# Four edits to the planner that orders a hybrid decoder step: product prices, a page slack, the moment of weight loads, a held accumulator

## The chip, the cores and the metric

The kernel runs on one core of one Trainium2 chip. The metric is device time in microseconds (us) of one launch, lower is better. The kernel before took 855.02 us as the median of three runs (854.64 to 855.18).

## What is computed

One layer of a decoder step for a prompt of 256 tokens and for 8 requests of 8 new tokens each, 320 token columns in all. Everything is float32. Cut to what matters here:

```python
z = x @ w_in                                    # 2048 x 8272, split among three head groups
# A: sparse attention, 8 heads x 128; an indexer scores all keys, the best 256 (64) are attended
sc  = sum_h w[t,h] * relu(q_idx[t,h] . k_idx[s]);  sel = top_k(sc)
a   = softmax(q . K[sel]) @ V[sel]              # for requests: K and V in 16 pages of 128 tokens each
# B: gated linear recurrence, 4 heads x 128
S_t = diag(f_t) S_{t-1} + outer(1 - f_t, i_t);  b = S_t^T q_t
# M: attention over 256 memory tokens, 4 heads; for the prompt their keys and values are products too
m   = softmax(q . mk) @ mv
y   = concat(a * silu(.), norm(b) * silu(.), m * silu(.)) @ w_out      # 2048 x 2048
out = layernorm(alpha * x + y)
```

The new keys, values, index keys, states and memory keys and values are outputs as well.

## The kernel before, in words

**Products.** TensorE multiplies in a fast float32 form. For accuracy each operand is split into a high and a low part (`xh`, `xl` for the activations, `wh`, `wl` for the weights), and each product is made of three: high by high, low by high, high by low. A weight tile of 128 x 1024 is loaded by SyncE's queue (SP) into one of three raw buffers `wr`; ScalarE casts each half of it to `wh`, VectorE or GpSimd subtracts to get `wl` (four buffers each, so four halves); then TensorE uses the half, which frees the buffer. One weight tile of the input projection gives 24 products of 320 columns (256 columns for the indexer's queries), in four quanta of six products. Order of the weights: a first block, queries, keys, values, the recurrence's inputs, gates, the memory weights (16 tiles, products of 512 and 256 columns), the memory queries, the last gates, and then the output projection in four chunks of 512 columns.

**Pages.** The requests' cached keys and values are read as pages of 128 x 1024. A "unit" is four pages, held in two buffers of the tag `pg` (five buffers) or `S` (three, shared with the score rows); TensorE reads the pages as moving operand of small matmuls, into the PSUM bank `kv` for scores and `va` for values. There are 68 units: eight for the keys and eight for the values of each of four request pairs, and four for the memory caches. TensorE visits them two at a time where it can.

**The order is written at build time by a planner.** The class `Plan` keeps a clock for each engine, for the SP queue and for the DMAs. Each instruction that the program emits is charged a cost (`Engine.cost`, line 188) and moves that engine's clock; `plan.w` and `plan.r` hold when each buffer was last written and read. The main loop goes step by step at `plan.now`, which follows TensorE's clock:

- `loads()` (line 2057) puts DMAs on SP's queue: a weight tile first if a raw buffer is about to be free (line 2065, up to 1 us ahead of it), then stores, then pages if a page buffer is free and the planned DMA clock is less than 4 us ahead.
- the weights' halves are prepared when they have landed and a `wh` buffer is free.
- `background()` (line 2021) advances generators (attention, recurrence, softmax and so on), each of which emits small matmuls, VectorE and ScalarE work when its inputs count as ready.
- then TensorE gets either a visit of one or two page units (`units_now`, line 800) or a quantum of products (`pe_quantum`, line 1686). If neither counts as ready, `plan.now` moves by 0.1 us and nothing is emitted.

So the planner's clock decides only the order of the instructions on each engine and queue. On the chip each engine runs its list in that order and waits on semaphores where the data are not there yet.

The helpers that the change touches: `unit_ready` (line 779) and `loaded` (line 797) say whether a unit's pages count as landed; `slot_free(tag, bufs)` (line 89) gives the planned time from which a new buffer of a tag may be taken, infinite if the buffers are pinned; `unit` (line 722) emits a unit's matmuls and for values takes the bank `va` at the first of eight units; `extract` (line 1262) reads that bank when all eight are done.

Of the kernel before, what the change touches and what calls it, by code (L numbers as in the profile page):

```python
# [45 lines left out]
HASTE = 2.0  # L46
CALM = 4.0
IDLE = 3.0
LOOK = 3
TABLES = {AF.Exp: "exp_ln", AF.Ln: "exp_ln", AF.Silu: "silu", AF.Sqrt: "sqrt"}  # L50
EXP_LN = 6
# [94 lines left out]
class Engine:  # L146
# [41 lines left out]
    def cost(self, op, outs, ins, n):  # L188
        if self.name == "PE":
            n, a = math.prod(outs[0].shape[1:]), ins[0]  # L190
            shape = tuple(next(w for w in (32, 64, 128) if m <= w) for m in (a.shape[0], math.prod(a.shape[1:])))
            turn = 0.0
            if shape != self.shape:
                turn = 0.31 if shape == (128, 128) else 0.09 if self.shape == (128, 128) else 0.2
                self.shape = shape
            if op == "transpose":
                return turn + 0.109
            if a.dtype == F32R:
                return turn + 0.0087 + n * 0.0004325
            if a.dtype == BF:  # L200
                return turn + max(0.06, n / 2400 + 0.003)
            if shape == (128, 32):
                return turn + max(0.028, n / 2400)
            return turn + 2 * max(0.109, n / 1200 + 0.002) * (0.5 if shape[0] == 64 else 1)
        scalars = sum(math.prod(x.shape[1:]) == 1 for x in ins) if n > 1 else 0
        sb = all(x.space != bass.MemoryType.PSUM for x in outs + ins)
        if self.name == "ACT":
            return ((112 if sb else 62) + n) / 1200 + 0.09 * scalars + (0.1 if len(outs) > 1 else 0)
        if self.name == "POOL":
            return (130 + 0.75 * n) / 960 if op in ("memset", "tensor_copy", "iota") else (170 + 2.0 * n) / 960  # L210
        f = 1.0
        if op in ("max", "match_replace"):
            return (66 + n) / 960 - 0.05
        if op == "tensor_tensor_scan":
            f = 2.0
        elif op in ("tensor_copy", "tensor_scalar", "memset") and sb:
            f = 0.55
        elif op == "reciprocal":
            f = 6.0
        return (66 + n * f) / 960 + 0.055 * scalars  # L220
# [8 lines left out]
def hymba_step(ctx: ExitStack, tc: tile.TileContext, I, O):  # L229
    nc = tc.nc  # L230
    plan = Plan()
# [60 lines left out]
    def PS(shape, which=None, dt=F32):  # L292
        if which is None:
            fa, fb = [(held[w] == 2, plan.slot_free(w, 2)) for w in ("mA", "mB")]
            which = "mA" if fa <= fb else "mB"
        return new(shape, which, dt, psum)
# [220 lines left out]
    wspec = []  # L517
# [204 lines left out]
    def unit(n):  # L722
        kind, p, u = punits[n]
        tl = [PG.pop((n, b)) for b in range(2)]
        plan.pinned.difference_update(t.tensor.name for t in tl)
        in_s.difference_update([(n, 0), (n, 1)])
        if kind == "K":
            if u == 0:
                S[p] = new([128, PAST + NS], "S")
                plan.pinned.add(S[p].tensor.name)  # L730
            if u % 2 == 0:
                st["kv"] = PS([128, 512], "kv")
            c = 256 * (u % 2)
            for hh in range(2):
                for h2 in range(2):
                    for b, hp, g in GROUPS:
                        h = 4 * hh + 2 * hp + h2
                        PE.matmul(st["kv"][g:g + 32, c:c + 256], st["qpad"][:, h, 2 * p + b, :],
                                  tl[b][:, :, 128 * h:128 * h + 128], start=hh == h2 == 0, stop=hh == h2 == 1)
            if u % 2:  # L740
                ps = st.pop("kv")
                plan.pinned.add(ps.tensor.name)
                bg.insert(0, [key_scores(p, u, ps), need(ps, ps=0)])
        elif kind == "V":
            if u == 0:
                VACC[p] = PS([128, 512], "va")
            for j in range(2):
                kt = 2 * u + j
                for b, hp, g in GROUPS:
                    PE.matmul(VACC[p][g:g + 32, :], PTt[p][:, kt, g:g + 32], pair(tl[b][:, j, :], hp),  # L750
                              start=kt == 0, stop=False)
            if u == 7:
                for b, hp, g in GROUPS:
                    PE.matmul(VACC[p][g:g + 32, :], PTt[p][:, 16, g:g + 32], pair(avS, hp),
                              start=False, stop=True)
                bg.insert(0, [extract(p), need(VACC[p], ps=0)])
                done.add(("vdone", p))
        elif kind == "XK":
            if p == 0:
                st["xk"] = PS([128, 512], "kv")  # L760
            ps = st["xk"][:, 256 * p:256 * p + 256]
            for h in range(4):
                for b in range(4):
                    PE.matmul(ps[32 * b:32 * b + 32, :], st["mqpad"][:, 4 * p + b, h, :],
                              tl[b // 2][:, b % 2, 256 * h:256 * h + 256], start=h == 0, stop=h == 3)
            if p == 1:
                for g in range(2):
                    bg.insert(0, [xsoft(g, st["xk"][:, 256 * g:256 * g + 256]), need(st["xk"], ps=0)])
        else:
            va = PS([128, 512], ("va", "kv")[p])  # L770
            for nt in range(2):
                for b in range(4):
                    PE.matmul(va[32 * b:32 * b + 32, :], st["xpt", p][:, nt, 32 * b:32 * b + 32],
                              tl[b // 2][:, b % 2, 512 * nt:512 * nt + 512], start=nt == 0, stop=nt == 1)
            bg.insert(0, [xextract(p, va), need(va, ps=0)])
            if p == 1:
                free(st["mqpad"])

    def unit_ready(n):
        kind, p, u = punits[n]  # L780
        if any((n, b) not in PG or plan.avail(PG[n, b]) > plan.now for b in range(2)):
            return False
        if kind == "K":
            return u % 2 or ("aq", 7) in done and plan.slot_free("kv", 1) <= plan.now and (
                u or plan.slot_free("S", BUFS["S"]) <= plan.now and len(S) + len(in_s) + ci_live(1) < BUFS["S"]
                and (p < BUFS["S"] or ("soft", p - BUFS["S"]) in done))
        if kind == "V":
            return ("soft", p) in done and plan.avail(PTt[p]) <= plan.now and (u < 7 or "attn" in done) and (
                u or plan.slot_free("va", 1) <= plan.now)
        if kind == "XK":  # L790
            return p or "mqpad" in done and "kv" not in st and plan.slot_free("kv", 1) <= plan.now
        return p or ("attn" in done and all(("xsoft", g) in done and plan.avail(st["xpt", g]) <= plan.now for g in (0, 1))
                     and max(plan.slot_free("va", 1), plan.slot_free("kv", 1)) <= plan.now)
# [1 line left out]
    since = [None]  # L795

    def loaded(n):
        return all((n, b) in PG and plan.avail(PG[n, b]) <= plan.now for b in range(2))

    def units_now(n):  # L800

# [460 lines left out]
    def extract(p):  # L1262
        while not has_room(2):
            yield
        o = [T(256), T(256)]
        for i in range(2):
            ACT.activation(o[i], VACC[p][:, 256 * i:256 * i + 256], AF.Copy, scale=RS[p][:, 1:2])
        del VACC[p], PTt[p]
        yield from wait(("gate", 7))
        yield need(*o)  # L1270
        ps = PS([128, 4, 128])
        for h4 in range(4):
            PE.transpose(ps[:, h4, :], o[h4 // 2][:, 128 * (h4 % 2):128 * (h4 % 2) + 128], ident)
        pv = ps.rearrange("p a (b h m q) -> p a b h m q", b=2, h=2, m=4)
        cv = st["cat"][0][:, 0:8, 256 + 16 * p:272 + 16 * p].rearrange("p (a h m) (b q) -> p a m b h q", a=2, h=2, b=2)
        for h4 in range(4):
            d = cv[:, h4 // 2, h4 % 2]
            DVE.tensor_mul(d, d, pv[:, h4, :, :, h4, :])
            for hp in range(2):
                cat_left["s", h4 // 2 * 4 + 2 * hp + h4 % 2] -= 1  # L1280
        free(*o)
# [775 lines left out]
    def loads():  # L2057
        nonlocal nw, npg
        while True:
            if plan.t["SP"] > plan.now + 0.5:  # L2060
                return
            if nw < len(wspec) and wspec[nw].get("ref"):
                nw += 1
                continue
            if nw < len(wspec) and nw < half + 5 and plan.slot_free("wr", 3) <= plan.now + 1 and nw - nprep < 3 \
                    and (wspec[nw]["kind"] != "mem" or has_room(3)):
                load_w(nw)
                nw += 1
                continue
# [202 lines left out]
```

## Time and profile before

| | |
|---|---|
| median of three runs | 855.02 us |
| the profiled execution's own time | 854.57 us |
| its span, first to last instruction | 852.8 us |
| granted TensorE clock, mean of the span | 0.997 |
| VectorE, ScalarE, GpSimd busy | 65%, 50%, 38% |
| bytes moved by DMA | 266.49 MB |

The 1.8 us between the profiled execution's time and its span lie before the first and behind the last instruction. Almost all compute instructions carry line 157, that of the wrapper which records them, so groups are told apart by the tiles they write and read (out<-in). In the view of the chain that ended last, each piece has its start, its length and the number of instructions; a length divided by that number is the spacing of back-to-back matmuls. A busy TensorE in the profile is a modelled one: a matmul's recorded duration (316 ns for 320 columns) overlaps the next one's.

### The profile page before, as it was taken

What the parts mean: (1) busy time and instruction counts of PE and PEld (TensorE: products, weight loads), DVE (VectorE), ACT (ScalarE), POOL (GpSimd) and SP (SyncE); (2) the same over time, 40 slices, a digit from 0 to 9 for tenths busy, and PEclk for the clock granted to TensorE, in tenths of its full rate; (3) what the DMA queues carried; (4) which work ended last, traced back from release to release, by engine and by line L of the source; (5) the groups of instructions that cost most, each with busy time, mean ns of one, the idle gap of its engine ahead of it and who ended that gap; (6) DMA issues with size and microseconds to landing.
All of it is one profiled execution on the core that took longest, in us unless ns stands there. A gap on an engine that the chain in (4) does not pass through costs nothing.

```text
span 852.8 us, 19150 instructions
## 1 busy us (share of the span) xinstructions
PE 843.1 (99%) x6892; PEld 718.0 (84%) x6892; DVE 553.9 (65%) x1100; ACT 422.3 (50%) x908; POOL 326.0 (38%) x333
## 2 busy tenths in 40 slices
PE   9999999999999999999999999999999999999996
PEld 8999999877889898878778788787887889888885
DVE  7788897744897898654474556557545343953655
ACT  6454565553555543634544554554444353744432
POOL 0677562564634445331142214333311110714424
PEclk9999999999999999999999999999999999999998
DMA  9567456889999999999989999999999988756633
GB/s 342 172 189 228 156 172 251 279 307 411 376 389 397 335 327 359 398 360 403 389 330 409 408 353 389 401 397 377 347 409 400 364 324 291 272 171 199 195 99 123
DMA packets 83216, 266.49 MB, mean 312 GB/s; under 512 B 10481, under 2 KB 21170, under 8 KB 82482
## 3 DMA queue, kind: packets, MB, share of 16 engines
q1 hardware_dynamic: 82098, 263.18, 83.6%
q0 software_dynamic: 1024, 2.10, 0.8%
q8 instruction: 54, 0.88, 0.4%
q14 instruction: 40, 0.33, 0.1%
HBM read 256.50 MB, written 8.73 MB: 311 GB/s over the span
## 4 chain that ended last, share of the span: by engine, by line
PE 98%; DMA 1%; DVE 0%; SPq 0%; ACT 0%; DVEq 0%; issue 0%
PE pj L157 57%; PE mB L157 13%; PE va L157 10%; PE mA L157 10%; PE kv L157 8%; DMA S<-in_first 1%; DVE pg L157 0%; SPq L157 0%; ACT xh L157 0%; ACT PT L157 0%; DVE s L157 0%; DVEq L2258 0%; DVE avn L157 0%
## 5 line engine op out<-in xcount | busy, mean ns | idle before, releaser
L157 ACT CAST wh<-wr 128x512 fp32r<-128x512 f32 x334 | 205.0, 621 | 243.5 <-PE pj L157 183.9
L157 PE MATMUL pj<-xh,wh 128*128 128x320 f32 (+1 forms) x992 | 313.6, 316 | 0.0
L157 PE MATMUL pj<-xh,wl 128*128 128x320 f32 (+1 forms) x992 | 303.9, 306 | 0.0
L157 PE MATMUL pj<-xl,wh 128*128 128x320 f32 (+1 forms) x992 | 303.8, 306 | 0.0
L157 DVE TENSOR_TENSOR wl<-wr,wh 128x512 fp32r<-128x512 f32 x222 | 172.7, 785 | 181.9 <-ACT wh L157 166.5
L157 POOL TENSOR_TENSOR wl<-wr,wh 128x512 fp32r<-128x512 f32 x112 | 151.0, 1357 | 240.2 <-ACT wh L157 222.7
L157 PEld LDWEIGHTS pj<-xh,wh 128*128 128x128 f32 x992 | 186.7, 188 | 16.0 <-issue 12.5
L157 PEld LDWEIGHTS pj<-xl,wh 128*128 128x128 f32 x992 | 186.8, 188 | 1.3
L157 PEld LDWEIGHTS pj<-xh,wl 128*128 128x128 f32 x992 | 186.6, 188 | 0.0
L157 POOL TENSOR_TENSOR t<-t,t 128x256 f32<-128x256 f32 (+3 forms) x53 | 46.2, 873 | 119.5 <-ACT t L157 60.0
L157 PE MATMUL va<-pg,PT 128*32 128x512 f32 x456 | 58.4, 595 | 0.0
L157 PE MATMUL kv<-pg,qpad 128*32 128x256 f32 (+1 forms) x916 | 57.5, 380 | 0.0
L157 PEld LDWEIGHTS kv<-pg,qpad 128*32 128x32 f32 (+1 forms) x916 | 30.8, 110 | 20.4 <-issue 1.3
L157 PEld LDWEIGHTS va<-pg,PT 128*32 128x32 f32 x456 | 14.6, 109 | 30.4 <-issue 28.1
L157 DVE MAX8 PT<-PT 128x8 f32<-128x1032 f32 x32 | 39.5, 1234 | 0.5
L157 DVE MATCH_REPLACE8 PT<-PT 128x1032 f32<-128x1032 f32 x32 | 39.0, 1218 | 0.0
L157 POOL DMA_INDIRECT S<-in_ci,row x24 | 25.5, 1064 | 20.0 <-DVE row L157 10.6
L157 PE MATMUL mB<-t,wh 128*128 128x256 f32 x128 | 24.5, 289 | 0.0
L157 POOL TENSOR_TENSOR bp<-t,bp 128x128 f32<-128x128 f32 (+1 forms) x17 | 10.7, 627 | 36.0 <-ACT bp L157 36.0
L157 DVE TENSOR_TENSOR cat<-S,cat 64x512 fp32r<-64x512 f32 x24 | 19.5, 813 | 6.9 <-ACT cat L157 6.4
L157 POOL TENSOR_TENSOR t<-t,tabm 128x320 f32<-128x320 f32 x16 | 14.5, 908 | 24.4 <-DVE t L157 24.2
L157 POOL TENSOR_TENSOR xl<-cat,xh 128x256 fp32r<-128x256 f32 x12 | 12.5, 1061 | 24.8 <-ACT xh L157 24.8
(430 smaller groups left out, 1355.0 us busy)
## 6 DMA issues: line engine op xcount, KB each, us to landing
wr<-in_wt SPq DMA_DIRECT2D x124, 512.0 KB
pg<-in_ck SPq DMA_DIRECT2D x114, 512.0 KB
pg<-in_cv SPq DMA_DIRECT2D x114, 512.0 KB
wr<-in_wo SPq DMA_DIRECT2D x36, 512.0 KB
wr<-in_wm SPq DMA_DIRECT2D x16, 512.0 KB
S<-in_ck SPq DMA_DIRECT2D x14, 512.0 KB
S<-in_cv SPq DMA_DIRECT2D x14, 512.0 KB
pg<-in_cXV SPq DMA_DIRECT2D x8, 512.0 KB
```

Source lines behind the costliest of these rows:

```text
L157: res = f(*a, **k)
```

## The change

Four edits, all in the planner or in what it asks; no instruction's operands, shapes or number of products are touched.

1. **Product prices.** A split product of n columns was counted at 0.0087 + n x 0.0004325 us, and is now counted at 0.0133 + n/2400: for 320 columns 0.1466 in place of 0.1471, for 256 columns 0.1200 in place of 0.1194, for 512 columns 0.2266 in place of 0.2301.
2. **Page slack.** A unit's pages count as landed 0.6 us (`PAGE_LAG`) after the planned landing, both for the first unit of a visit and for the second.
3. **Weight loads.** A weight tile's DMA is put on SP's queue when the raw buffer is free by the plan, no longer up to 1 us ahead of that.
4. **Held accumulator.** The bank `va` is pinned from the first value unit of a request pair until `extract` has emitted its reads, so that `slot_free("va", 1)` is infinite in between.

```diff
+PAGE_LAG = 0.6
...
-                return turn + 0.0087 + n * 0.0004325
+                return turn + 0.0133 + n / 2400
...
                 VACC[p] = PS([128, 512], "va")
+                plan.pinned.add(VACC[p].tensor.name)
...
     def unit_ready(n):
         kind, p, u = punits[n]
-        if any((n, b) not in PG or plan.avail(PG[n, b]) > plan.now for b in range(2)):
+        if not loaded(n):
             return False
...
     def loaded(n):
-        return all((n, b) in PG and plan.avail(PG[n, b]) <= plan.now for b in range(2))
+        return all((n, b) in PG and plan.avail(PG[n, b]) + PAGE_LAG <= plan.now for b in range(2))
...
             ACT.activation(o[i], VACC[p][:, 256 * i:256 * i + 256], AF.Copy, scale=RS[p][:, 1:2])
+        plan.pinned.discard(VACC[p].tensor.name)
         del VACC[p], PTt[p]
...
-            if nw < len(wspec) and nw < half + 5 and plan.slot_free("wr", 3) <= plan.now + 1 and nw - nprep < 3 \
+            if nw < len(wspec) and nw < half + 5 and plan.slot_free("wr", 3) <= plan.now and nw - nprep < 3 \
```

## The prediction

> **What bounds the kernel now.** I read the profile's page first: its span, its first line of busy times and the chain that ended last.
>
> ```profile
> span 852.8 us, 19150 instructions
> PE 843.1 (99%) x6892; PEld 718.0 (84%) x6892; DVE 553.9 (65%) x1100; ACT 422.3 (50%) x908; POOL 326.0 (38%) x333
> PE 98%; DMA 1%; DVE 0%; SPq 0%; ACT 0%; DVEq 0%; issue 0%
> ```
>
> TensorE is busy for 99% of the span and is 98% of the chain. Busy time is modelled, so I look for waiting directly: TensorE's waits of the whole span.
>
> ```profile
> PE kv L1947 <- DVE t L157: 1.1, 1, 1.1
> PE va L157 <- ACT PT L157: 0.6, 1, 0.6
> ```
>
> These two are all there are above 0.15 us, and both lie in the start-up. No wait for a page and none for a weight stands there. The third view cuts the span into stages, one row each: length, busy time of TensorE, weight loads, VectorE, ScalarE and GpSimd, then granted clock, DMA share and GB/s.
>
> ```profile
> 210.00:348.00 138.00, 138.00 (x1353) 121.42 (x1352) 115.46 (x196) 71.41 (x168) 65.79 (x50) 1.00 0.97 367
> 348.00:475.00 127.00, 127.00 (x1175) 100.24 (x1173) 70.25 (x146) 58.72 (x130) 33.49 (x43) 1.00 0.99 381
> 533.00:600.00 67.00, 67.00 (x572) 52.65 (x565) 44.06 (x88) 35.76 (x81) 24.18 (x25) 1.00 1.01 393
> 600.00:708.00 108.00, 108.00 (x925) 86.08 (x925) 50.49 (x128) 50.11 (x129) 19.99 (x23) 1.00 0.96 361
> 728.00:845.00 117.00, 116.83 (x545) 97.47 (x543) 69.78 (x116) 54.67 (x106) 49.47 (x40) 1.00 0.54 169
> 847.00:849.00 2.00, 0.00 (x0) 0.00 (x0) 2.00 (x4) 0.19 (x1) 0.00 (x0) 0.74 1.00 406
> 849.00:851.00 2.00, 0.00 (x0) 0.00 (x0) 0.64 (x2) 0.00 (x0) 0.00 (x0) 0.50 0.60 232
> ```
>
> In the page stages TensorE is busy for every microsecond at full clock, beside DMAs that are 96 to 101% busy; in the output projection it idles 0.17 us of 117. Whatever a planner puts in another order, the same matmuls remain. So the time can fall only by what is not a matmul's own time, and rise by any wait that a new order makes.
>
> **Part 1, prices.** Pieces of the chain (start, length, what, count) give the real spacing.
>
> ```profile
> 272.17 7.92 PE pj L157 x54
> 555.39 1.44 PE mB L157 x12
> 556.83 1.39 PE pj L157 x6
> 793.64 1.36 PE va L157 x6
> ```
>
> 7.92/54 = 0.1467 us for 320 columns, 1.44/12 = 0.1200 for 256, 1.36/6 = 0.2267 for 512. The new prices (0.1466, 0.1200, 0.2266) are these; the old ones were 0.1471, 0.1194 and 0.2301. The edit costs nothing on the chip, it moves the planner's clock: by groups of the same shape,
>
> ```profile
> L157 PE MATMUL pj<-xh,wh 128*128 128x320 f32 x896 | 286.3, 320 | 0.0
> L157 PE MATMUL mB<-wh,xh 128*128 128x512 f32 x54 | 21.0, 389 | 0.0
> ```
>
> three times 896 products become 0.0005 us shorter each, 1.3 us in all by the output projection; each group of 54 wide ones takes off another 54 x 0.0035 = 0.19 us after it. That is one or two quanta of six products (0.88 us each) in 728 us, spread thin. Value on the chip: 0.0. Bounds: the 0.17 us idle of the projection could go, or as much come.
>
> The Trainium skill states another spacing ("TensorE: Matmul & The Clock Gate", section "Back-to-back issue gap": columns/2.4 plus 2.5 ns), which gives 135.8 ns for 320 columns; by it even the new price is 10.8 ns too long, the planner would lag behind the chip, pages would be visited early; the sum would stay, but I would put a tenth more of the chances on slower. The measured 0.1467 us decides against it, and the chances below do not use it.
>
> **Part 2, page slack.** The visits' pieces, and the weight loads' waits of the whole span:
>
> ```profile
> 626.19 1.85 PE va L157 x16
> 629.11 1.85 PE va L157 x16
> 644.13 3.57 PE va L157 x32
> ...
> PEld va L157 <- DMA pg<-in_cv: 0.8, 3, 0.3
> ```
>
> A full value visit is 32 matmuls in 3.57 us. The weight loads at its head were held by a page's landing three times, 0.3 us at most, hidden beside running products, since TensorE's own list has no such wait. So pages land in time, three times barely; the slack of 0.6 us protects a margin that is not yet spent, and its direct gain is 0. It postpones a visit by 0.6 us, in steps of a quantum (0.88 us); in between TensorE does products that it must do anyway. What it can lose: page buffers are given back up to 0.9 us later. The DMAs are 96 to 101% busy there, with weights and other pages queued, so they have other work for that long. One visit stands split: two pieces of 16 in 1.85 us, 2 x 1.85 - 3.57 = 0.13 us more than one, plus the way back to products. That way back:
>
> ```profile
> 697.48 0.38 PE L157 MATMUL mB<-ident,t 128*128 128x128 f32 x2
> 697.61 0.39 PE L157 MATMUL pj<-xh,wh 128*128 128x320 f32 x1
> 697.84 0.30 PE L157 MATMUL pj<-xl,wh 128*128 128x320 f32 x1
> 697.99 0.31 PE L157 MATMUL pj<-xh,wl 128*128 128x320 f32 x1
> ...
> 285.66 6.36 PE pj L157 x42
> ```
>
> After transposes the first product takes 697.84 - 697.61 = 0.23 us in place of 0.15: a return costs 0.08 us. After a visit the 42 products take 6.36 us against 42 x 0.1467 = 6.16: 0.20 us with the way in. A split visit thus costs 0.13 + 0.20 = 0.33 us. With the first unit also made to wait, a pair is split only if the first has been ready for long; I take half a split away, -0.15 us (bounds -0.33 for the one gone, +0.66 for two new ones).
>
> **Part 3, weight loads.** SyncE's queue waits, whole span:
>
> ```profile
> SPq L157 <- DVE wl L157: 154.2, 79, 6.3
> SPq L157 <- POOL wl L157: 129.3, 54, 6.5
> ```
>
> SP stands 283 us, 133 times and 2.1 us each, in front of a weight load whose raw buffer is still being read by the subtraction. All that is behind it waits too: pages, stores, page numbers. Asked 1 us later, the load goes on the queue behind what was ready meanwhile. Its own issue does not come later by that, as it waits for the same release; but a page that now stands ahead takes its share of the DMAs. A unit's buffer is two DMAs of 512 KB, 2 x 524,288 bytes at 393 GB/s = 2.67 us. Who waits for the weight then? ScalarE's cast, then the subtraction, then TensorE. The row of the casts among the costliest groups:
>
> ```profile
> L157 ACT CAST wh<-wr 128x512 fp32r<-128x512 f32 x334 | 205.0, 621 | 243.5 <-PE pj L157 183.9
> ```
>
> Of 243.5 us idle before casts, 183.9 were ended by TensorE giving back a `wh` buffer: the landed weight waits for TensorE, not the reverse. So most landings may slip by 2.67 us. Value 0.0; bounds -0.2 (the projection's idle) to the price of the slower rival.
>
> **Part 4, held accumulator.** `slot_free("va", 1)` is asked for the next pair's first value unit, which also needs that pair's softmax, and for the memory values. Both come later than the reads:
>
> ```profile
> 670.99 4.43 PE va L157 x40
> 675.42 1.06 PE mB L157 x4
> ...
> 702.25 1.85 PE va L157 x16
> ```
>
> The last pair's final visit ends at 675.42, the next user of the bank starts at 702.25, 27 us later. The pin costs 0 while those reads are emitted within that time, and cannot gain. If the reads were late by more, the memory values would move behind further products, again 0.
>
> **Re-made order.** The four together shift which small groups fall between which products. Each return is 0.08 us; no row tells how many will be added or saved, so I allow for ten either way, -0.8 to +0.8, value 0.
>
> **Sum.** 0 - 0.15 + 0 + 0 + 0 on the profiled execution's own 854.57 us (span 852.8 and 1.8 around it): 854.4. That execution lies 0.45 us under the median of the runs, 855.02, so for the median of the changed kernel 854.9 us. Bounds of the terms added in the same direction: -0.17 - 0.33 - 0.2 - 0.8 = -1.5 and 0.17 + 0.66 + 0.8 = +1.6, which is 853.5 to 856.6.
>
> **Rivals.** *Faster by bundling.* If small groups meet at the same step, 25 returns fewer give 25 x 0.08 = 2.0 us, the split visit 0.33, the projection's idle 0.17: 2.5 us, 852.5. For it: truer prices and the slack hold visits until more is ready. Against it: the groups are set by chains of results, and 25 is a large part of what a 1 us shift touches.
>
> *Slower by pages ahead of weights*, in the memory weights, 533 to 600 us. There the casts already wait for landings (ScalarE's waits, 210 to 600 us):
>
> ```profile
> ACT wh L157 <- DMA wr<-in_wm: 6.3, 4, 2.0
> ```
>
> A tile there lasts 1.39 + 1.44 = 2.83 us on TensorE, with DMAs 101% busy. In four of 16 tiles the cast waited, up to 2.0 us, without TensorE waiting. If a page buffer's 2.67 us goes ahead in those four, at least 0.67 us each and at most 2.67 reach TensorE: 2.7 to 10.7 us. It decides where the halves prepared ahead cover less than 2.67 us more; since 243.5 us of idle casts speak for cover, I take the low end, 857.7. For it: this is what the edit of the load does on SP. Against it: TensorE may visit the pages that came earlier.
>
> *Slower by the clock.* After the last matmul the granted clock is 0.74 in the slice from 847 to 849 and 0.50 in the next, so some 3 us without matmuls halve it. One wait of that length would cost itself and as much again in slow products, 6 us: 861. Nothing in the waits comes near it. The Trainium skill (same page, "What's actually happening") gives the idle window as about 3.4 us, which agrees.
>
> *The change does nothing*: if every decision falls as before, the order is the same and the time 855.0. It lies within the forecast.
>
> **How the numbers follow.** About 0.2% (1.7 us) is what a measurement here can tell from no change. Forecast with the case of no effect 0.65: all its bounds lie within 1.7 us. Bundling 0.16. Pages ahead of weights 0.16 and the clock 0.03, together 0.19. The range takes in the forecast's bounds and reaches into either rival for about half of its chance, 852.9 to 857.6; the likeliest case's own is 853.5 to 856.6.
>
> **What would show it.** Right: TensorE's waits still without pages and weights, 100% busy stages, SP's 283 us in front of weight loads much smaller, value visits all of 32 or 40 matmuls, the projection's stage still ending within 1 us of 845. Wrong: entries of `wl` or `wh` among TensorE's waits in 533 to 600 us, idle time in the stage rows, or many more 16-matmul visits; on the other side, clearly fewer small pieces between the products in the chain, with the last matmul before 843.5.

## The result and the profile after

The changed kernel takes 864.07 us (median of 6 runs, 862.46 to 866.62) against 855.07 us for the kernel before on the same chip (854.64 to 855.5, 6 runs): a ratio of 1.0111, 95% interval 1.0093 to 1.0128. It is 9.0 us slower; the forecast was no change, and the time lies above the range. The profiled execution took 865.99 us, one of the longer ones; spans are compared with the 852.8 us of before.

The top of the page of after, and its first line on the chain that ended last:

```profile
span 864.2 us, 19138 instructions
...
PE 848.0 (98%) x6892; PEld 722.2 (84%) x6892; DVE 550.2 (64%) x1099; ACT 424.7 (49%) x910; POOL 327.7 (38%) x334
...
PE 94%; DMA 3%; DVE 1%; SPq 1%; ACT 0%; issue 0%; POOL 0%; DVEq 0%
```

The matmuls are the same 6892, but the chain, 98% TensorE and 1% DMA before, now has 3% of DMA and 1% of VectorE in it. What TensorE waits for in after (us in total, times, longest):

```profile
PE mB L158 <- ACT t L158: 3.4, 1, 3.4
PE kv L158 <- DMA pg<-in_ck: 3.3, 1, 3.3
PE kv L1950 <- DVE t L158: 1.1, 1, 1.1
PE va L158 <- ACT PT L158: 0.5, 1, 0.5
```

The last two are the old ones (1.1 and 0.6 before). The first two are new, 6.7 us together: a transpose waits for ScalarE, a page visit for a page. The stages in which they lie, with two-microsecond slices after each (start:end, length, busy time of PE, PEld, DVE, ACT and POOL, granted clock, DMA share, GB/s):

```profile
348.00:475.00 127.00, 127.00 (x1167) 102.84 (x1169) 67.31 (x138) 57.66 (x123) 34.73 (x44) 1.00 0.99 382
475.00:533.00 58.00, 55.08 (x549) 46.04 (x541) 33.10 (x72) 29.39 (x66) 15.29 (x16) 1.00 0.97 364
533.00:600.00 67.00, 66.60 (x578) 53.35 (x578) 37.54 (x81) 34.21 (x78) 22.64 (x25) 0.97 0.97 365
600.00:708.00 108.00, 104.61 (x867) 83.05 (x870) 51.72 (x116) 48.57 (x123) 21.40 (x27) 0.97 0.95 359
534.00:536.00 2.00, 2.00 (x23) 0.80 (x12) 0.00 (x0) 0.00 (x0) 0.00 (x0) 0.60 1.03 410
606.00:608.00 2.00, 2.00 (x11) 1.57 (x14) 1.97 (x3) 0.40 (x1) 0.00 (x0) 0.50 1.01 395
```

From 348 to 475 us TensorE is as full as before. Then it idles 2.9 us, 0.4 us and 3.4 us in three stages that had no idle time, and the granted clock, 1.00 there before, falls around both waits: the trace's record of the clock has 0.5 from 534.39 us for 3.41 us and from 602.65 us for 6.83 us. The timeline of TensorE in after (start, us, instruction, and in brackets the idle time before it):

```profile
334.57 2.80 PE L158 MATMUL kv<-pg,qpad 128*32 128x256 f32 x48
...
529.45 0.63 PE L158 MATMUL kv<-pg,qpad 128*32 128x256 f32 x4
533.40 2.71 PE L158 MATMUL kv<-pg,qpad 128*32 128x256 f32 x28 [3.33 <-DMA pg<-in_ck]
...
603.67 0.90 PE L158 MATMUL mB<-ident,t 128*128 128x128 f32 x3 [3.39 <-ACT t L158]
...
604.64 0.47 PE L158 MATMUL pj<-xl,wh 128*128 128x320 f32 x1
604.90 0.47 PE L158 MATMUL pj<-xh,wl 128*128 128x320 f32 x1
```

and the same visits before:

```profile
330.10 3.66 PE L157 MATMUL kv<-pg,qpad 128*32 128x256 f32 x64
...
529.72 3.66 PE L157 MATMUL kv<-pg,qpad 128*32 128x256 f32 x64
```

Three things are read here. The visit at 330.10 us starts at 334.57, 4.5 us later, though the slack is 0.6 us: a visit starts only where a tile of products begins, so what misses one start waits for the next. At 529 us before, units 6 and 7 of the last key pair were one visit of 64; after, unit 6 is visited alone (4 and 28), its page isn't there, and unit 7 follows later by itself. And at half clock the products start every 0.267 us in place of 0.147, so 45% of such time is lost.

The account: waits 8.3 - 1.7 = 6.6 us more; half clock 0.45 x 3.41 = 1.5 us in the first stretch and 0.45 x 5.8 = 2.6 in the second, of whose 6.83 us TensorE still waits 1.0. Together 10.7 of the 11.4 us by which the span grew. This is the account of one execution, and a long one. Its mean granted clock is 0.991; in the five others it is 0.994 or 0.995, at spans of 860.7 to 864.9 us. They had less time at half clock, and yet one of them is longer: for the median the half clock weighs less than here, and other times vary from run to run.

**The page wait, followed back.** The chain of waits in after around it:

```profile
523.49 9.78 DMA pg<-in_ck
```

The page was asked for at 523.5 us and came at 533.3. SyncE's queue between 500 and 534 us, first its longest wait, of after

```profile
SPq L158 <- DVE wl L158: 8.2, 1, 8.2
```

and of before

```profile
SPq L157 <- DVE wl L157: 6.7, 3, 5.7
```

and its timeline in after:

```profile
500.34 0.85 SPq L158 DMA_DIRECT2D S<-in_ck  x2
509.51 0.34 SPq L158 DMA_DIRECT2D wr<-in_wt  x1
...
513.91 4.67 SPq L158 DMA_DIRECT2D pg<-in_ck  x6
...
522.33 1.50 SPq L158 DMA_DIRECT2D pg<-in_ck  x2
```

and in before:

```profile
494.91 1.17 SPq L157 DMA_DIRECT2D pg<-in_ck  x2
...
505.65 0.86 SPq L157 DMA_DIRECT2D S<-in_ck  x2
...
515.92 1.81 SPq L157 DMA_DIRECT2D pg<-in_ck  x2
```

From 501.2 to 509.5 us SyncE stood before one weight load, whose raw buffer VectorE was still to read, and the pages stood behind it; the DMAs ran almost dry, at 20 GB/s from 509 to 510 us against 418 from 505 to 507. But this stand is only a part of the delay. Counted back from the last page, the three rows of before ask for the second buffer of the last pair's unit 4, the first of unit 5 and the second of unit 6, which is the one waited for; after, the same requests start at 500.34, 513.91 and 522.33 us. So the pages were asked for 5.4 us late before SyncE stood, 8.3 us late behind the stand, and 6.4 us late at the end. The planner does not see the stand: it counts a raw buffer that has landed as free although nothing has read it yet. Over the whole span SyncE's waits in after are

```profile
SPq L158 <- DVE wl L158: 174.5, 84, 8.2
SPq L158 <- POOL wl L158: 118.9, 46, 6.5
```

293 us in place of 283: the edit of the weight loads did not shorten them, nor did it alone (287.5 us in loads_alone).

**The transpose's wait, followed back**, in the chain of after:

```profile
599.61 1.37 DVE wl L158
600.98 1.48 DVE t L158
...
602.88 0.34 DVE t L158
603.24 0.38 ACT t L158
```

The transposes of the recurrence need a bank `mB`; both banks hold the memory keys until they are copied out, the last two lines. VectorE comes to that copy late, behind a subtraction of 1.37 us and a step of the recurrence of 1.48. The planner took a bank for free that nobody had read: the two accumulators are allocated one after the other before either is written, and its list then drops the first one for the second.

### The profile page after: what moved, and what is told of

It reads as the page before. It is cut to its first block, busy times and chain, and to the rows that moved or that the text cites. A ratio compares the mean times of both kernels' runs of the same rounds, so it can differ in the third digit from the quotient of the medians.

```text
span 864.2 us, 19138 instructions
## 1 busy us (share of the span) xinstructions
PE 848.0 (98%) x6892; PEld 722.2 (84%) x6892; DVE 550.2 (64%) x1099; ACT 424.7 (49%) x910; POOL 327.7 (38%) x334
## 4 chain that ended last, share of the span: by engine, by line
PE 94%; DMA 3%; DVE 1%; SPq 1%; ACT 0%; issue 0%; POOL 0%; DVEq 0%
PE pj L158 54%; PE mB L158 12%; PE va L158 10%; PE mA L158 9%; PE kv L158 8%; DMA pg<-in_ck 2%; DMA pg<-in_cv 1%; DMA S<-in_first 1%; SPq L158 1%; DVE pg L158 0%; DVE t L158 0%; DVE wl L158 0%; ACT wh L158 0%; POOL t L158 0%; ACT t L158 0%
## 5 line engine op out<-in xcount | busy, mean ns | idle before, releaser
L158 POOL TENSOR_TENSOR wl<-wr,wh 128x512 fp32r<-128x512 f32 x111 | 148.2, 1341 | 254.2 <-ACT wh L158 211.8
L158 POOL TENSOR_TENSOR t<-t,t 128x256 f32<-128x256 f32 (+3 forms) x56 | 49.9, 891 | 128.1 <-DVE t L158 56.8
L158 DVE TENSOR_TENSOR cat<-S,cat 64x512 fp32r<-64x512 f32 x24 | 17.1, 714 | 9.7 <-ACT cat L158 9.2
```

The source lines that it names most:

```text
L158: res = f(*a, **k)
```

## The experiments

The theory: a new order brings waits that the planner does not see, because it holds pages and buffers for ready that are not; the waits and the half clock behind them are the loss. The rivals: one of the edits costs by itself (the slack by late visits, the weight loads by standing behind pages). In the table, waits are the sum of the rows of TensorE's waits, and half is the time at half clock before the last matmul, both of the profiled execution. Each ratio is to the kernel before on the same chip, whose median was 854.86 to 855.15 us in these comparisons; differences in the text are to the medians of the table.

| kernel | median us | ratio to before, 95% | span | waits | half |
|---|---|---|---|---|---|
| before | 855.07 | | 852.8 | 1.7 | 0 |
| the change | 864.07 | 1.0111 (1.0093 to 1.0128) | 864.2 | 8.3 | 10.2 |
| p_alone | 858.74 | 1.0045 (1.0030 to 1.0060) | 856.6 | 3.3 | 0 |
| slack_alone | 861.14 | 1.0071 (1.0048 to 1.0093) | 858.7 | 4.9 | 3.4 |
| loads_alone | 858.68 | 1.0042 (1.0031 to 1.0054) | 854.9 | 3.3 | 0 |
| prices_slack | 864.95 | 1.0116 (1.0093 to 1.0139) | 861.9 | 8.7 | 3.4 |
| pair_k3 | 862.76 | 1.0088 (1.0072 to 1.0104) | 860.8 | 7.6 | 3.4 |
| fill_k3 | 877.75 | 1.0258 (1.0245 to 1.0272) | 876.3 | 5.1 | 3.4 |
| fill_8 | 864.10 | 1.0113 (1.0098 to 1.0128) | 862.1 | 4.7 | 3.4 |
| slack_3us | 866.52 | 1.0128 (1.0113 to 1.0142) | 865.3 | 7.8 | 6.8 |
| true_raw | 859.43 | 1.0047 (1.0030 to 1.0065) | 857.8 | 4.1 | 0 |
| bank_taken | 862.37 | 1.0091 (1.0075 to 1.0106) | 860.6 | 6.3 | 3.4 |
| pair_and_bank | 859.84 | 1.0057 (1.0044 to 1.0071) | 855.8 | 3.7 | 0 |
| price_up | 856.74 | 1.0023 (1.0013 to 1.0032) | 854.8 | 3.4 | 0 |
| truth_after | 858.06 | 1.0037 (1.0023 to 1.0050) | 858.8 | 5.1 | 0 |
| truth_before | 860.86 | 1.0071 (1.0057 to 1.0084) | 859.1 | 4.3 | 0 |

**One edit alone.** The held accumulator alone gives the same program as before, instruction for instruction, and the change without it the same program as the change; so it is no part of the cause. The other three, each put alone into the kernel before, and two of them together:

*p_alone*, the prices only:

```
-                return turn + 0.0087 + n * 0.0004325
+                return turn + 0.0133 + n / 2400
```

> The kernel before with the new product prices alone. Theory (a lone visit meets pages that have not landed): its order also parts the last two key units of the fourth pair at the start of the memory weights, so TensorE should wait there, 2 to 5 us with the slow clock behind it: 857 to 864 us. Rival (the page slack delays visits): no slack here, so 855.0 within 0.5. Rival (weight loads behind pages): loads as before, so 855.0 within 0.5.

858.74 us. TensorE's waits that before has not:

```profile
PE pj L157 <- ACT t L157: 0.8, 1, 0.8
PE mA L157 <- ACT t L157: 0.5, 1, 0.5
```

A few tenths here and there, no page, no half clock, and 3.7 us slower. The time lies in the theory's range, but not for its reason: units 6 and 7 are parted here too (visits of 32 at 529.43 and 534.31 us), and no page is waited for.

*slack_alone*, the slack only:

```
+    return all((n, b) in PG and plan.avail(PG[n, b]) + PAGE_LAG <= plan.now for b in range(2))
```

> The kernel before with the page slack of 0.6 us alone. Theory (a lone visit): the same two units are parted, with four more lone visits behind them: 858 to 866 us. Rival (the slack itself): 860 to 866 us, all of the loss. Rival (weight loads behind pages): 855.0 within 0.5.

861.14 us, which lies in the range of the theory and in that of the slack itself. The lone visit and its page wait are there:

```profile
PE kv L158 <- DMA S<-in_ck: 3.0, 1, 3.0
```

TensorE's instructions come in the order of before up to the visit of 330.10 us. That is the first one which the slack puts off: it starts at 334.72 us.

*loads_alone*, the weight loads only:

```
-  ... and plan.slot_free("wr", 3) <= plan.now + 1 and ...
+  ... and plan.slot_free("wr", 3) <= plan.now and ...
```

> The kernel before with weight loads queued at the planned release alone. Its visits are paired as in the kernel before. Theory (a lone visit): 855.0 within 0.7. Rival (the slack itself): 855.0 within 0.5. Rival (weight loads behind pages): all of the loss, 860 to 866 us.

858.68 us, over the theory's 855. The visit that starts at 231.46 us before is planned a tile earlier here, and its second page isn't there; its rows in the timeline:

```profile
227.89 2.35 PE L157 MATMUL kv<-pg,qpad 128*32 128x256 f32 x36
231.77 1.92 PE L157 MATMUL kv<-pg,qpad 128*32 128x256 f32 x28 [1.53 <-DMA pg<-in_ck]
```

The profiled execution was the fastest of its ten (856.69 us); what the others wait for beyond this is not seen.

*prices_slack*, these two edits together:

> The kernel before with prices and slack, loads as before. Its visits are paired as in the changed kernel. Theory (a lone visit): the changed kernel's time, 862 to 867 us. Rival (weight loads behind pages): 855.0 within 0.5. Rival (the slack itself): 860 to 866 us.

864.95 us, the time of the whole change (the slack's own range reaches up to 866 and holds it too), with both long waits:

```profile
PE kv L158 <- DMA pg<-in_ck: 3.5, 1, 3.5
PE mB L158 <- ACT t L158: 3.4, 1, 3.4
```

So no single edit is guilty: each of the three re-orders the kernel and each loses 3.6 to 6.1 us, with other waits in other places; prices and slack together are the whole loss, and the weight loads add nothing that shows on top. Nor do the losses add up: 13.4 us for the three alone, 9.0 for all at once.

**Curing the page wait.** *pair_k3*, the change with one rule more:

```
+        if kind == "K" and p == 3 and half < 130:
+            return 0
```

> The changed kernel, with one line more: a key unit of the last pair of heads is never visited alone while the memory weights start, so K3.6 and K3.7 are planned as one visit, as in the kernel before. Theory (two waits of TensorE, each with a stretch at half clock, carry the loss): the page wait of 3.3 us and the 1.7 us that its half clock costs are gone, 864.1 - 5.0 = 859.1 us (857.5 to 861), no clock of 0.5 near 530 us. Rival (visits later by a tile everywhere; the page wait takes the place of a wait that would come anyway): 864 within 1.5.

862.76 us: the page wait is gone, but of the 5.0 us expected at most 1.3 came back, and the intervals of the two kernels overlap. One long wait stays and one is new:

```profile
PE mB L158 <- ACT t L158: 3.3, 1, 3.3
PE mA L158 <- ACT kN L158: 1.3, 1, 1.3
```

TensorE's waits for `PT` are 1.7 us here and 0.5 in the change. They lie in the first 12 us, before the edited step, where the two programs are the same, so about a microsecond of the waits varies between executions and is not due to the edit.

*fill_k3*, products of no use to keep TensorE busy while the page comes:

```
+            if p == 3 and u == 6:
+                for f in range(42):
+                    nc.tensor.matmul(st["kv"][0:32, 0:256], st["qpad"][:, 0, 0, :],
+                                     st["qpad"][:, 0].rearrange("p a c -> p (a c)"), start=True, stop=True)
```

> The changed kernel, with 42 products of zero use put before the lone visit of K3.6, written by hand past the planner, so that the order of all else stays; the first real product clears what they leave. TensorE is busy while the page comes. Theory (the idle time brings the half clock, and the half clock has a price of its own): no 0.5 near 534 us, 1.7 us less than the changed kernel, plus at most 0.7 where the products run longer than the wait: 862.4 to 863.1 us. Rival (the wait alone costs, the half clock falls on time that is lost anyway): 864.1 to 864.8 us, whatever the clock shows.

877.75 us. The 42 products took 18 us, not the 4 that I had reckoned:

```profile
529.15 18.10 PE L737 MATMUL kv<-qpad 128*32 128x256 f32 x83
```

so this run says nothing of the half clock. *fill_8*, with `range(8)`:

> As the kernel with 42 products before the lone visit of K3.6, now with 8, at the 0.43 us that each of the 42 took in one group of columns: 3.4 us, about the page wait of 3.3 us. Theory (the half clock after an idle stretch has a price of its own): no 0.5 near 534 us, no page wait, 864.1 - 1.7 + 0.1 = 862.5 us (861.7 to 863.3). Rival (the wait alone costs): 864.2 us (863.6 to 865).

864.10 us, the rival's number. Yet its profile has what the theory asked for: a wait of 0.2 us where 3.3 was, and the 28 products of the visit in 1.92 us in place of 2.71.

```profile
529.64 3.42 PE L737 MATMUL kv<-qpad 128*32 128x256 f32 x15
...
533.94 1.92 PE L158 MATMUL kv<-pg,qpad 128*32 128x256 f32 x28 [0.22 <-DMA pg<-in_ck]
```

Its span is 2.1 us under that of the change, its median equal, while the change's own runs spread over 4.2 us. That half clock stretches products is seen in the rows; that this stretch costs 1.5 us of the median is not shown.

**A larger slack.** *slack_3us*: `PAGE_LAG = 3.0`.

> The changed kernel with a slack of 3.0 us in place of 0.6. Theory (the loss is in pages that land later than planned, by up to 4.6 us): page waits are at most 1.6 us, 857 to 862 us. Rival (the slack itself costs, by putting off visits and giving back page buffers later): more than the changed kernel, 866 to 870 us, without a large wait of TensorE.

866.52 us. No key page is waited for any more; two cross-attention pages are, and a chain over VectorE makes a wait with 6.8 us at half clock behind it:

```profile
PE mA L158 <- DVE s L158: 3.1, 1, 3.1
PE kv L158 <- DMA pg<-in_cXV: 1.7, 2, 1.5
```

The theory's time is missed and the rival's number is met, but not in the rival's manner: there is a large wait, of another kind.

**Telling the planner the truth.** *true_raw*, a raw weight buffer counts as taken from its load until it is prepared:

```
+        plan.pinned.add(WR[i].tensor.name)
...
+                if WR.get(nprep) is not None:
+                    plan.pinned.discard(WR[nprep].tensor.name)
```

> The changed kernel, but the planner counts a raw weight buffer as taken from its load until it has been prepared, so that it issues a weight load only where SyncE will not stand. Theory (SyncE stands up to 8.2 us before a weight load with pages behind it, and the planner doesn't see it): SyncE's longest wait before a weight load falls under 3 us, no page wait of TensorE over 1 us, 857 to 861 us. Rival (the stand of SyncE doesn't matter, the order is as good or bad as any): 861 to 868 us.

859.43 us, 4.6 us under the change, with no page among TensorE's waits, none over

```profile
PE mB L158 <- POOL t L158: 1.2, 1, 1.2
```

and no half clock. SyncE's longest wait before a weight load fell to 6.3 us only, not under 3, so that the pages come in time is shown, and that it is by the shorter stand is not.

*bank_taken*, the accumulators of the memory weights count as taken until they are copied out:

```
+                pj["m"] = []
+                for w in ("mB", "mB", "pj", "pj"):
+                    pj["m"].append(PS([128, 512], w))
+                    plan.pinned.add(pj["m"][-1].tensor.name)
...
+        plan.pinned.difference_update(t.tensor.name for t in acc)
```

> The changed kernel, but the planner also counts the four accumulators of the memory weights as taken from the first product until the step that copies them out, as the change does for the value accumulators. Theory (the wait of 3.4 us near 600 us is a transpose planned into a bank of mB that the planner took for free and whose copies were still to come): that wait and its half clock are gone, 864.1 - 5.5 = 858.6 us (857 to 860.5), the page wait near 530 us stays. Rival (VectorE and ScalarE are late there whatever bank is used, the wait only moves): 862 us or more, a wait of 2 us or more between 595 and 640 us.

862.37 us. The transposes wait no longer, but a wait of 1.4 us stands on a later use of `mB`, and only 1.7 us came back of the 5.5 expected, with intervals that overlap. The rival's number is met, its wait of 2 us or more is not there:

```profile
PE kv L158 <- DMA pg<-in_ck: 3.0, 1, 3.0
PE mB L158 <- ACT t L158: 1.4, 1, 1.4
```

*pair_and_bank*, this with the paired visit:

> The changed kernel with both: K3.6 and K3.7 in one visit, and the accumulators of the memory weights taken until read. Theory: both long waits and all half clock before the end are gone, 862.8 - 5.0 = 857.8 us (856.5 to 859.5). Rival (each cure brings a wait elsewhere): 861 us or more.

859.84 us. Both long waits and the half clock are gone; the longest that is left beside the old ones is

```profile
PE mA L158 <- ACT kN L158: 1.1, 1, 1.1
```

It is 4.2 us faster than the change, with intervals apart, as it should be if the two waits are part of the cause. But a cure is a new order too, and 4.8 us of loss remain, more than the theory left there and less than the rival; and orders with no new wait over 1.5 us lose 3.6 and 3.7 us (loads_alone, p_alone).

*truth_after*, the change with both beliefs put right (raw buffers and accumulators):

> The changed kernel with both of the planner's false beliefs put right: raw weight buffers taken until prepared, and the accumulators of the memory weights taken until copied out. Theory A (the two beliefs are the whole cause): the rest of the loss goes too, 854.5 to 857 us. Theory B (they are two of many: in each order other than the one before, page landings and chains over VectorE and ScalarE miss the plan by a microsecond or two in places, which costs some 4 us): 857.5 to 861 us, with two to five waits of 0.3 to 1.5 us.

858.06 us, theory B. Three late pages and a chain over GpSimd:

```profile
PE kv L158 <- DMA pg<-in_ck: 1.3, 3, 0.7
PE mB L158 <- POOL t L158: 1.1, 1, 1.1
```

**Re-ordering for other reasons.** *price_up*, the kernel before with the prices moved as far the other way:

```
-                return turn + 0.0087 + n * 0.0004325
+                return turn + 0.0041 + n * 0.0004483
```

> The kernel before, one edit: the planner's price of the large products is moved as far as the change moves it, but the other way (320 columns: 147.1 to 147.6 ns instead of 146.6; 512 columns: 230.1 to 233.6 instead of 226.6). Theory (any other order draws waits that the plan doesn't see, the direction of the edit hardly matters): slower, 857 to 863 us, with new waits of TensorE. Rival (the change's prices are the wrong way: TensorE planned faster than it runs puts visits ahead of their pages): 853.5 to 855.5 us.

856.74 us, slower by 0.23%, between the two expectations, with two new waits of 0.7 and 0.5 us, the longer being

```profile
PE mB L157 <- ACT PT L157: 0.7, 1, 0.7
```

So the sign fits the theory, and the size differs: 1.7 us here, 3.7 with the change's prices. *truth_before*, the kernel before with both beliefs put right and nothing else:

> The kernel before with the same two beliefs put right, and no other edit. Theory A: no worse than before, 853 to 855.5 us. Theory B (the order before is one in which almost nothing misses, and any other loses): slower than before, 857 to 861 us, though the planner knows more.

860.86 us, theory B, with short waits for GpSimd, VectorE and pages, for example

```profile
PE mA L157 <- DVE t L157: 1.0, 1, 1.0
```

None of the kernels beats the one before. Every order other than its own was slower, by 0.2 to 1.3% without the added products, whether the planner was told more, less or something else.

## Why the prediction was wrong

**Prices.** Right that the new prices are the measured spacing, and that the edit costs nothing on the chip itself. Wrong that its value is therefore 0: alone it costs 3.7 us (858.74), through the order, the only thing that it changes. The 135.8 ns that the prediction sets beside the measured spacing is no rule for this kernel: the Trainium skill ("TensorE: Matmul & The Clock Gate", "Back-to-back issue gap") gives that formula for an isolated matmul. Here each of the 6892 matmuls has a weight load.

**Page slack.** This step failed first: "It postpones a visit by 0.6 us, in steps of a quantum (0.88 us)". The step is a tile: the visit of 330.10 us went to 334.57, and with the slack alone to 334.72 (with the prices alone to 329.80). The bound "page buffers are given back up to 0.9 us later" is too small for the same reason: the visits of 503.39 and 515.38 us start at 506.15 and 522.14 in after, and the pages were asked for 5.4 us late even ahead of SyncE's long stand. The term for split visits, -0.15 us, had the wrong sign: one key visit more is split (529.45 and 542.68 us), which by the prediction's own 0.33 us is a loss. Last, "the slack protects a margin that is not yet spent" was true of the order before and of no other: with the slack in place the longest page wait was 3.0 us (slack_alone).

**Weight loads.** The price of a page ahead, 2.67 us, was not what was paid, and no weight is among TensorE's waits. What the trace shows is the reverse: pages behind a weight load, 8.2 us at one stand. I had the row of SyncE's 283 us and read it as something that the edit would shorten; it grew to 293.

**Held accumulator.** Right: without effect.

**Re-made order.** "no row tells how many will be added or saved, so I allow for ten either way, -0.8 to +0.8": this is the term of the sum that was wrong by its size. It priced the order by returns of 0.08 us, when the same paragraphs had said that the time can rise by any wait that a new order makes. Three edits alone measured +3.6, +3.7 and +6.1 us there, with single waits of up to 3.0 us; the waits hold 1.6, 1.6 and 3.2 us of it.

**The rivals.** *Slower by the clock* had the price of a long wait nearly right: 6 us, where the account above has 3.3 + 1.5 and 3.4 + 2.6; it happened twice. What would bring such a wait it did not say. It got 0.03 because "nothing in the waits comes near it", which asks the order before about waits of an order that does not exist yet. *Pages ahead of weights* did not occur. *Faster by bundling* neither: no order here came out faster.

**What stays open.** With both long waits cured, 3 to 5 us of loss remain. The waits listed account for 2.0 of the 3.0 us by which the span is longer in pair_and_bank, 1.6 of 3.8 in p_alone and 2.6 of 6.3 in truth_before; the rest has no row among the waits. In p_alone a key visit and a value visit more than before are split in two, at 0.33 us each by the prediction's price some 0.7 us of the rest; in pair_and_bank no visit is split. The other runs of pair_and_bank are longer than the profiled one by up to 3.2 us, while 50 of 55 executions of before lie between 854.4 and 855.7 us; that pages land a little differently in each run and meet thin margins is a guess. Nor do the runs tell why the order before alone has almost no waits.

## What to carry to other kernels

Where a program orders a kernel by planned times, an edit of its prices or margins is a new order, and is to be priced by the waits that an order can have, not by the edit: three small edits cost 0.4 to 0.7% each here, in different places. A margin at a decision that is only taken at tile starts moves the work by tiles. Before trusting a plan, look for what it counts as free when it is only landed or not yet written: here raw weight buffers and two accumulators; with both put right the change got back 6.0 of its 9.0 us, though the same cure made the kernel before 5.8 us slower. So it is not shown that a truer plan is a faster one: each of these kernels is one more order.

## What the runs showed of the hardware

The half clock comes in whole pieces. Ahead of the last matmul its stretches lasted 3.41 or 6.83 us, and the two of after begin 602.65 - 534.39 = 68.26 us apart, 20.0 pieces. The Trainium skill ("TensorE: Matmul & The Clock Gate", "What's actually happening") describes such a free-running window of 3413 ns, with the clock halved after an idle window; the lengths and the distance agree. A whole idle window was not needed, though: the window from 530.98 to 534.39 us still held the first 1.0 us of the visit. In slack_alone 2.2 us of idle time were enough (TensorE waits from 530.18 to 533.18 us, the stretch begins at 532.36). And a wait of the same length can go without it, as in prices_slack, whose transposes wait 3.39 us up to 603.99 us, with the clock at 1.00 in the slice behind:

```profile
604.00:606.00 2.00, 2.00 (x15) 2.00 (x15) 1.97 (x2) 1.22 (x3) 1.08 (x1) 1.00 0.98 391
```

Counted on from that run's stretch at 534.11 us, a window ends at 602.37 us and parts this wait into 1.8 and 1.6 us. That neither part was enough would fit; it is one case. So the price of a wait of 3.4 us is not one number: it brought none, one or two such pieces (prices_slack, fill_8, the change).

The filling products, 32 rows of output by 256 columns, all write the same 32 rows of the bank: 83 recorded matmuls in 18.10 us, 0.218 us each. 28 of the visit's, whose outputs take turns over four such sets of rows, took 1.92 us, 0.069 each. So the filling products cost three times what I had taken from the visit; that the shared rows are the reason is not shown by itself.
